# Rotated queries and keys written to DRAM head by head, 32 rows in a transfer

## The chip, the cores and the metric

The kernel runs on one core of a Trainium2 chip. The metric is the device time of one execution in microseconds (us). Three runs of the kernel before gave a median of 3471.29 us (3470.65 to 3471.43).

The core has five engines with instruction queues of their own: PE (TensorE: matmuls and transposes), DVE (VectorE), ACT (ScalarE), POOL (GpSimd) and SP (SyncE). In this kernel every transfer between SBUF and DRAM is issued by SP, in the order of SP's instructions, and moved by the core's 16 DMA engines.

## The reference

A sequence of 2048 tokens with 1024 features goes through two blocks. The first is a gated short convolution and then an attention layer with "stick-breaking" weights. The second is the block that the change touches. Cut to what matters:

```python
h = rms_norm(x, norm_w) * (1 + scale) + shift            # scale, shift, gate from c
u_pool, g_pool, q, k, v, g_attn, qi, ki, wi = split(h @ w_in)
pool_out = pool_mixer(u_pool) * silu(g_pool)
q  = rope(rms_norm(q, q_norm_w))      # 8 heads of 64
k  = rope(rms_norm(k, k_norm_w))      # 2 heads of 64
qi = rope(qi)                         # 8 index heads of 64
ki = rope(ki)                         # 1 index head of 64

def rope(x):                          # rotates the two halves of each head
    x1, x2 = x[..., :32], x[..., 32:]
    return concat([x1 * cos - x2 * sin, x2 * cos + x1 * sin])

def dsa_attention(q, k, v, qi, ki, wi):    # per block of 128 queries
    score = sum_h(relu(qi_h @ ki.T) * wi_h)          # causal
    sel = top_k(score, 256)
    o = softmax(q @ k[sel].T / 8) @ v[sel]

x = x + gate * (concat([pool_out, attn_out]) @ w_out)
```

## The kernel before

The sequence is worked in two halves h of HT = 1024 tokens. Features lie on the 128 partitions, tokens along the row, so a tile of 128 features of one half is 128 rows of 4 KB (512 KB). Matrix products with float32 accuracy take three matmuls per block of weights (`lin`, L112 to L122: high by high, high by low, low by high); a full product of 1024 features and one half is 48 matmuls of 512 columns.

The stages are generators that yield their estimated cost; `merge` (L56) interleaves two of them so that both move in proportion to given totals. A scheduling layer then orders each engine's instructions; the order is fixed when the program is built. The stages by letters:

- `phase_a`, `phase_b`: the convolution block and the projections of the first attention. `phase_c(h)`: stick-breaking attention; it loads queries (`crr<-qst`), keys (`crr<-kst`) and values (`crf<-vst`) through small rings of buffers.
- `phase_d(h)`: output projection of the first block and the norm before the second. `phase_e(h)` (L682): the projections `ki`, `k`, `v`, `qi`, `q`, with rope, written to DRAM for later. `phase_e2`: gates and the pool mixer.
- `f_setup(h)` (L836) loads the second block's keys into SBUF (`keys<-kis`, `keys<-k2s`, `keys<-v2s`), after a small POOL copy (L842). `phase_f`: index scores (L871, L872), top-k search on DVE and ACT, attention (L1147 to L1194); its queries come in as `ffr<-qis` and `ffr<-q2s`. `phase_g`: the last projection.

Around the change, `phase_c(1)` runs merged with `phase_d(0)`, `phase_e(0)`, `phase_e2` of half 0 (L1308, some 1500 to 2100 us into the run), and `phase_d(1)`, `phase_e(1)` run merged with the first part of `phase_f` (L1318, some 2100 to 2500 us).

Rope is in two helpers. `rope_pair` (L646) takes two tiles x and y, the first and second halves of four heads, each 4 heads by 32 rows, and makes four tiles: high and low parts of both results, in the buffers `rb`, `ra`, and twice `xe`. Each of the four goes to DRAM in one transfer of 128 rows (L661). It is called twice per half for `qi` (into `qis`) and twice for `q` (into `q2s`): 32 transfers of 512 KB in all. `rope` (L627) does the same within one tile for `ki` (one head, 32 rows in a transfer of 128 KB, into `kis`) and for `k` (two heads, 64 rows in a transfer of 256 KB, into `k2s`), from the buffers `sw` and `xe`. There are 8 transfers into `k2s` and 8 into `kis`.

Weights of the second half's projections were kept in DRAM by the first half and come back as `fixedr<-kept_w_in`, two transfers of 512 KB for 48 matmuls, into a ring of four buffers (L89), so a load waits until PE has left its buffer.

Completion of SP's transfers is counted in eight semaphores (DMAHW0 to DMAHW7 in the listings below), given out in turn: a transfer that takes a semaphore waits until the transfer that had it before, eight earlier, has landed.

Of the kernel before, what the change touches and what calls it, by code (L numbers as in the profile page):

```python
# [37 lines left out]
def merged(*gens):  # L38

    live = [[0.0, float(total), g] for g, total in gens]  # L40
    while live:
        live.sort(key=lambda e: e[0] / e[1])
        try:
            step = next(live[0][2])
            live[0][0] += step
            yield step
        except StopIteration:
            live.pop(0)


def run(gen):
    for _ in gen:
        pass


def merge(*gens):  # L56
    run(merged(*gens))


def until(gen, stop):  # L60

    while not stop():
        try:
            yield next(gen)
        except StopIteration:
            return


class Build:
# [557 lines left out]
    def rope(self, xe, half, dst):  # L627

        nc = self.nc
        sw = self.t4("sw")[:, :HT]  # L630
        one, two = slice(0, half), slice(half, 2 * half)
        self.dma(sw[one], xe[two])
        self.dma(sw[two], xe[one])
        x, w = xe[: 2 * half], sw[: 2 * half]
        nc.vector.tensor_tensor(x, x, self.cos[: 2 * half], ALU.mult)
        nc.vector.tensor_tensor(w, w, self.sin[: 2 * half], ALU.mult)
        nc.vector.tensor_tensor(x[one], x[one], w[one], ALU.subtract)
        nc.vector.tensor_tensor(x[two], x[two], w[two], ALU.add)
        nc.scalar.activation(w.bitcast(F32R), x, AF.Copy)
        nc.vector.tensor_tensor(x.bitcast(F32R), x, w, ALU.subtract)  # L640
        dst = dst.rearrange("(a t d) s n -> t a d s n", t=2, d=32)
        for t, rows in enumerate((one, two)):
            for i, y in enumerate((w, x)):
                self.dma(dst[t][:, :, i], y[rows])

    def rope_pair(self, x, y, dst):  # L646

        nc = self.nc
        a, b = self.t4("ra")[:, :HT], self.t4("rb")[:, :HT]
        nc.vector.tensor_tensor(a, x, self.cos, ALU.mult)  # L650
        nc.vector.tensor_tensor(b, y, self.sin, ALU.mult)
        nc.vector.tensor_tensor(a, a, b, ALU.subtract)
        nc.scalar.activation(b.bitcast(F32R), a, AF.Copy)
        nc.vector.tensor_tensor(a.bitcast(F32R), a, b, ALU.subtract)
        nc.vector.tensor_tensor(y, y, self.cos, ALU.mult)
        nc.vector.tensor_tensor(x, x, self.sin, ALU.mult)
        nc.vector.tensor_tensor(y, y, x, ALU.add)
        nc.scalar.activation(x.bitcast(F32R), y, AF.Copy)
        nc.vector.tensor_tensor(y.bitcast(F32R), y, x, ALU.subtract)
        for t, i, z in ((0, 0, b), (0, 1, a), (1, 0, x), (1, 1, y)):  # L660
            self.dma(dst[:, t, :, i].rearrange("d a n -> a d n"), z)  # L661

    def head_ms(self, ps, ind, before=None):

# [613 lines left out]
    def build(self):  # L1278
        tc, nc = self.tc, self.nc
        self.scores, self.masks, self.guess, self.r1 = {}, {}, {}, {}  # L1280
        self.kit, self.k2t, self.v2t = {}, {}, {}
        self.exact = False
        self.attended = 0
        self.e1 = self.e2 = False
        self.seen = {}
        pool = tc.tile_pool
        two = lambda a, b: [[i, i + 1] for i in range(a, b, 2)]
        with (
            pool(name="dr", bufs=1, space=DRAM) as self.dr,
            pool(name="cp", bufs=1) as self.cp,  # L1290
            pool(name="sm", bufs=2) as self.sm,
            pool(name="pw", bufs=2) as self.pw,
            pool(name="wk", bufs=1) as self.wk,
            pool(name="xa", bufs=8) as xa,
            pool(name="xb", bufs=8) as xb,
            pool(name="at", bufs=1) as self.at,
            pool(name="xg", bufs=1) as xg,
            pool(name="ps", bufs=1, space=PSUM) as self.ps,
        ):
            self.setup()  # L1300
            self.wide = True
            run(self.phase_a(0, xa, xb))
            merge((self.phase_a(1, xa, xb), 420), (self.adaln(), 9))
            run(self.phase_b(0, xa))
            self.wide = False
            merge((self.phase_b(1, xb), 167), (self.ahead(self.phase_c(0), 2000), 95))
            de = self.chain(self.phase_d(0, xb), lambda: self.phase_e(0), lambda: self.phase_e2([0, 1], self.h2))
            merge((self.ahead(self.phase_c(1), 2000), 260), (de, 300))  # L1308
            self.f_setup(0)
            f = self.phase_f([[b, b + 1] for b in range(0, 16, 2)])  # L1310
            de = self.chain(
                self.phase_d(1, xb),
                lambda: self.phase_e(1),
                lambda: self.f_setup(1) or (),
                lambda: self.phase_e2([2, 3], self.h2),
                lambda: self.done_e2() or (),
            )
            merge((de, 300), (until(f, lambda: self.e2), 230))  # L1318
            g = lambda q: self.chain(
                self.wait(lambda: self.attended >= 4 * q + 4), lambda: self.phase_g(q, xg, self.seen[4 * q + 3])  # L1320
            )
            fill = self.chain(g(0), lambda: g(1), lambda: g(2))
            merge((self.ahead(f, 0), 500), (fill, 400))
            run(self.phase_g(3, xg, self.seen[15]))
            ps = self.bank()
            nc.vector.tensor_tensor(self.dropped, self.dropped, self.due, ALU.not_equal)
            nc.tensor.matmul(ps[0:1, 0:16], self.ones[:, 0:1], self.dropped, start=True, stop=True)
            tot = self.small("tot", 2)[0:1, 0:1]
            nc.vector.tensor_reduce(tot, ps[0:1, 0:16], mybir.AxisListType.X, ALU.add)
            flag = self.small("tot", 2, I32)[0:1, 0:1]  # L1330
            nc.vector.tensor_copy(flag, tot)

            failed = nc.values_load(flag, min_val=0, max_val=P * 16)
            with tc.If(failed > 0):
                self.exact = True
                for h in range(2):
                    self.f_setup(h)
                run(self.phase_f(two(0, 16)))
            with tc.If(failed > 0):
                for q in range(4):  # L1340
                    run(self.phase_g(q, xg))
# [102 lines left out]
```

## Time and profile before

| | |
|---|---|
| Median of the runs | 3471.29 us |
| Profiled execution, its own time | 3474.31 us |
| Span of that execution, first to last instruction | 3472.6 us |
| Granted TensorE clock, mean over the span | 0.962 of full speed |
| Busy: PE, DVE, ACT, POOL | 93%, 65%, 43%, 14% |
| DMA | 438.66 MB, mean 126 GB/s |

A row of the timeline gives the start in us from the span's start, the duration, the engine, the source line, the operation, what it writes and reads (out<-in), and in square brackets how long the engine had been idle before it and what ended that. A row of the waits gives who waited for what: the sum in us, how often, and the longest. A row of the windows gives for one stretch its length, each engine's busy time and number of instructions, the granted TensorE clock, the mean busy share of the 16 DMA engines, and the GB/s that they moved. A "SPq DMA_DIRECT2D" row is the time that SP took to issue transfers, not the time that they took to land.

### The profile page before, as it was taken

Reading aid. Unit: us, or ns where it says so; the run is one execution under the profiler, and the core shown is the slowest. Engines: PE = TensorE matmul, PEld = TensorE weight load, DVE = VectorE, ACT = ScalarE, POOL = GpSimd, SP = SyncE. Lnnn points to the kernel's source line nnn. Section 1 sums busy time; section 2 is a strip of 40 time slices with the busy share of each in tenths; the row PEclk is TensorE's granted clock in tenths of the full one; section 3 lists DMA queues with packets and bytes.
Section 4 is the critical chain, followed back from the end, with each engine's and each line's share of the span. In section 5 each row is a group of like instructions: output and inputs, shape, how many; then the busy total and the mean of one; then the engine's idle time right before and its main releaser. Section 6 shows DMA issues by size and latency. Waiting matters only on the chain. (4 is left out here: it accounts for less than half of the span.)

```text
span 3472.6 us, 49120 instructions
## 1 busy us (share of the span) xinstructions
PE 3222.2 (93%) x17922; PEld 2569.6 (74%) x17922; DVE 2256.2 (65%) x4508; ACT 1482.4 (43%) x2668; POOL 484.3 (14%) x600
## 2 busy tenths in 40 slices
PE   8999999999999999988989998899898898889897
PEld 7888888888787777766767776677676676667675
DVE  5343544553535887788777787897447569888641
ACT  4111421111323444555545555563364365865561
POOL 0000110000100000142021112420200422102002
PEclk9999999999999999989999999899899999989999
DMA  3111442343464545645445444644433542115005
GB/s 108 49 47 52 157 160 83 127 131 107 143 173 140 173 130 153 200 152 139 145 152 178 131 133 137 191 149 145 153 104 107 164 158 95 47 43 174 25 29 174
DMA packets 369231, 438.66 MB, mean 126 GB/s; under 512 B 23504, under 2 KB 269776, under 8 KB 368976
## 3 DMA queue, kind: packets, MB, share of 16 engines
q1 hardware_dynamic: 368976, 435.38, 40.1%
q8 instruction: 145, 2.38, 0.3%
q14 instruction: 110, 0.90, 0.1%
HBM read 308.94 MB, written 124.78 MB: 125 GB/s over the span
## 5 line engine op out<-in xcount | busy, mean ns | idle before, releaser
L119 PE MATMUL lin<-act,fixedr 128*128 128x512 f32 x1488 | 603.6, 406 | 23.5 <-DMA fixedr<-kept_w_in 12.1
L120 PE MATMUL lin<-act,fixedr 128*128 128x512 f32 x1488 | 601.3, 404 | 12.8 <-DVE act L620 10.8
L121 PE MATMUL lin<-act,fixedr 128*128 128x512 f32 x1488 | 598.1, 402 | 0.0
L104 ACT ACTIVATE fixedr<-fixed 128x512 fp32r<-128x512 f32 x295 | 186.9, 634 | 730.0 <-PE lin L120 249.3
L548 DVE TENSOR_TENSOR_SCAN crf<-crf 128x512 f32<-128x512 f32 (+3 forms) x320 | 355.5, 1117 | 64.0 <-ACT crf L545 60.9
L119 PEld LDWEIGHTS lin<-act,fixedr 128*128 128x128 f32 x1488 | 286.8, 193 | 92.2 <-DMA fixedr<-kept_w_in 10.1
L120 PEld LDWEIGHTS lin<-act,fixedr 128*128 128x128 f32 x1488 | 286.0, 192 | 80.5 <-DVE act L620 14.9
L105 DVE TENSOR_TENSOR fixedr<-fixed,fixedr 128x512 fp32r<-128x512 f32 x295 | 204.3, 693 | 204.3 <-ACT fixedr L104 192.7
L121 PEld LDWEIGHTS lin<-act,fixedr 128*128 128x128 f32 x1488 | 285.8, 192 | 63.2
L1149 DVE CUSTOM_DVE_ANT_0 fe<-z,masks 128x512 f32<-128x512 f32 (+3 forms) x320 | 186.8, 606 | 151.7 <-PE z L1148 107.2
L557 ACT COPY crf<-tp 128x512 f32<-128x512 f32 (+3 forms) x320 | 164.5, 532 | 184.0 <-PE tp L555 166.9
L119 PE MATMUL z<-act,fixedr 128*128 128x512 f32 x584 | 231.1, 396 | 10.9 <-ACT fixedr L104 10.9
L538 ACT ACTIVATE crf<-z 128x512 f32<-128x512 f32 (+3 forms) x320 | 174.9, 548 | 136.3 <-PE tp L555 114.4
L121 PE MATMUL z<-act,fixedr 128*128 128x512 f32 x584 | 229.8, 394 | 0.0
L120 PE MATMUL z<-act,fixedr 128*128 128x512 f32 x584 | 229.7, 394 | 0.0
L1172 ACT COPY ff<-tp 128x512 f32<-128x512 f32 (+3 forms) x320 | 160.1, 522 | 156.6 <-PE tp L1170 89.4
L551 POOL TENSOR_TENSOR crf<-crf 128x1 f32<-128x1 f32 x192 | 89.0, 465 | 967.0 <-ACT crf L538 696.7
L881 DVE SCALAR_TENSOR_TENSOR sc<-ff,fixed,sc 128x512 f32<-128x512 f32 (+3 forms) x266 | 176.7, 686 | 59.4 <-ACT ff L874 58.5
L1170 PE MATMUL tp<-fixed,fe 128*128 128x128 f32 x1088 | 185.4, 292 | 30.9 <-ACT fe L1161 21.1
L874 ACT ACTIVATE ff<-z 128x512 f32<-128x512 f32 (+3 forms) x304 | 157.2, 544 | 128.9 <-PE z L872 120.8
L549 DVE TENSOR_TENSOR crf<-crf 128x511 f32<-128x511 f32 (+3 forms) x320 | 200.5, 632 | 11.2 <-DVE crf L548 0.5
L1161 ACT ACTIVATE fe<-fe,fixed 128x128 f32<-128x128 f32 (+15 forms) x128 | 165.7, 1295 | 76.6 <-DVE fixed L1160 75.8
(343 smaller groups left out, 6559.4 us busy)
## 6 DMA issues: line engine op xcount, KB each, us to landing
fixed<-in_w_in_a_dram SPq DMA_DIRECT2D x128, 256.0 KB
fixedr<-kept_w_out SPq DMA_DIRECT2D x64, 512.0 KB
kept_w_in<-fixedr SPq DMA_DIRECT2D x46, 512.0 KB
fixedr<-kept_w_in SPq DMA_DIRECT2D x46, 512.0 KB
crr<-kst SPq DMA_DIRECT2D x80, 256.0 KB
crr<-qst SPq DMA_DIRECT2D x64, 256.0 KB
fixed<-x2d SPq DMA_DIRECT2D x64, 256.0 KB
ffr<-q2s SPq DMA_DIRECT2D x128, 128.0 KB
```

The lines of the kernel that those rows point to most:

```text
L104: nc.scalar.activation(t[:, 0], raw, AF.Copy)
L105: nc.vector.tensor_tensor(t[:, 1], raw, t[:, 0].bitcast(F32), ALU.subtract)
L119: self.nc.tensor.matmul(ps[:, :n], whi[k], a, start=k == 0, stop=False)
L120: self.nc.tensor.matmul(ps[:, :n], whi[k], b, start=False, stop=False)
L121: self.nc.tensor.matmul(ps[:, :n], wlo[k], a, start=False, stop=k == nk - 1)
L538: nc.scalar.activation(s[:, :W], z[:, :W], AF.Sigmoid)
L548: nc.vector.tensor_tensor_scan(er, er, er, left, ALU.mult, ALU.min)
L549: nc.vector.tensor_tensor(s[:, : W - 1], s[:, : W - 1], e[:, 1:W], ALU.mult)
L881: nc.vector.scalar_tensor_tensor(sc[:, c0 : c0 + m], r[:, :m], w, sc[:, c0 : c0 + m], ALU.mult, ALU.add)
L1149: nc.vector.tensor_tensor_reduce(row[:, c0 : c0 + m], z[:, :m], mb[:, c0 : c0 + m], 1.0, NEG, ALU.subtract, ALU.max, mx[:, c : c + 1])
L1161: nc.scalar.activation(row[:, :W], row[:, :W], AF.Exp, bias=nbs, scale=sc, accum_out=den[:, hd : hd + 1])
L1170: nc.tensor.transpose(tp[:, j * P : (j + 1) * P], pe[a][:, k0 : k0 + P], self.ident)
```

## The change

`rope_pair` writes each of its four tiles in four transfers of 32 rows (128 KB), one for each head, instead of one transfer of 128 rows. `rope` does the same: the two heads of `k` go in two transfers of 32 rows instead of one of 64; for `ki`, which has one head, the transfers stay as they were. The places in DRAM and the bytes are the same. SP gets 104 transfers more: 128 for 32 from `rope_pair`, 16 for 8 from `rope`. The total given for `phase_c(1)` in one merge goes from 260 to 250.

```diff
@@ rope
         dst = dst.rearrange("(a t d) s n -> t a d s n", t=2, d=32)
-        for t, rows in enumerate((one, two)):
+        for t in range(2):
             for i, y in enumerate((w, x)):
-                self.dma(dst[t][:, :, i], y[rows])
+                for a in range(half // 32):
+                    r0 = t * half + 32 * a
+                    self.dma(dst[t][a][:, i], y[r0 : r0 + 32])
@@ rope_pair
         for t, i, z in ((0, 0, b), (0, 1, a), (1, 0, x), (1, 1, y)):
-            self.dma(dst[:, t, :, i].rearrange("d a n -> a d n"), z)
+            for hd in range(4):
+                self.dma(dst[:, t, hd, i], z[32 * hd : 32 * hd + 32])
@@ build
-            merge((self.ahead(self.phase_c(1), 2000), 260), (de, 300))
+            merge((self.ahead(self.phase_c(1), 2000), 250), (de, 300))
```

Three places of SP's order show what moves. The sizes at the end of a row's names are the shape that the transfer writes; in brackets is what it waits for. The first place is the first pair of `qi` in half 0. Before:

```order
668 L77 DMA qis_187<-rb 4x32x1024 [waits Activation_49]
669 L77 DMA qis_187<-ra 4x32x1024 [waits DMAHW4_49,DVE_49]
670 L77 DMA qis_187<-xe 4x32x1024 [waits Activation_49]
671 L77 DMA qis_187<-xe 4x32x1024 [waits DMAHW6_49,DVE_49]
672 L77 DMA fixed<-in_w_in_dram 128x4x128 [waits DMAHW7_49,DVE_49]
673 L77 DMA kept_w_in_0_12249<-fixedr 128x1024 [waits DMAHW0_49]
```

With the change, the same place on SP:

```order
676 L77 DMA qis_187<-ra 32x1024 [waits DMAHW3_49,DVE_49]
677 L77 DMA qis_187<-ra 32x1024 [waits DMAHW4_49]
678 L77 DMA qis_187<-ra 32x1024 [waits DMAHW5_49]
679 L77 DMA qis_187<-ra 32x1024 [waits DMAHW6_49]
680 L77 DMA qis_187<-xe 32x1024 [waits DMAHW7_49,Activation_49]
681 L77 DMA qis_187<-xe 32x1024 [waits DMAHW0_49]
682 L77 DMA qis_187<-xe 32x1024 [waits DMAHW1_49]
683 L77 DMA qis_187<-xe 32x1024 [waits DMAHW2_49]
684 L77 DMA qis_187<-xe 32x1024 [waits DMAHW3_49,DVE_49]
```

Each transfer is now four, and each of them takes a semaphore in turn, so the ninth of a pair waits for the first to land; the place in the program is the same.

The second place is the second pair of `qi` in half 0, and the four loads of queries for `phase_c(1)` near it. Before, on SP:

```order
686 L77 DMA qis_187<-ra 4x32x1024 [waits DMAHW5_49,DVE_49]
687 L77 DMA crr<-kst_0_149 64x2x512 [waits DMAHW6_49,PE_49]
688 L77 DMA crr<-kst_0_149 64x2x512 [waits DMAHW7_49]
689 L77 DMA qis_187<-xe 4x32x1024 [waits DMAHW0_49,DVE_49]
690 L77 DMA fixed<-in_w_in_dram 128x4x128 [waits DMAHW1_49,DVE_49]
691 L77 DMA kept_w_in_0_12667<-fixedr 128x1024 [waits DMAHW2_49]
692 L77 DMA crr<-qst_1_158 64x2x512 [waits DMAHW3_49,PE_49]
693 L77 DMA crr<-qst_1_158 64x2x512 [waits DMAHW4_49]
694 L77 DMA crr<-qst_1_158 64x2x512 [waits DMAHW5_49,PE_49]
695 L77 DMA crr<-qst_1_158 64x2x512 [waits DMAHW6_49]
```

With the change, from the first two of the query loads to the last two:

```order
706 L77 DMA crr<-qst_1_158 64x2x512 [waits DMAHW1_49,PE_49]
707 L77 DMA crr<-qst_1_158 64x2x512 [waits DMAHW2_49]
708 L77 DMA qis_187<-ra 32x1024 [waits DMAHW3_49,DVE_49]
...
719 L77 DMA qis_187<-xe 32x1024 [waits DMAHW6_49]
720 L77 DMA fixed<-in_w_in_dram 128x4x128 [waits DMAHW7_49,DVE_49]
721 L77 DMA kept_w_in_0_12635<-fixedr 128x1024 [waits DMAHW0_49]
722 L77 DMA crr<-qst_1_158 64x2x512 [waits DMAHW1_49,PE_49]
723 L77 DMA crr<-qst_1_158 64x2x512 [waits DMAHW2_49]
```

Two of the query loads now stand ahead of 12 of the writes (rows 708 to 719), the other two behind all 16 of the pair.

The third place is the end of `phase_e(1)`, where `f_setup(1)` loads the keys. Before, on SP:

```order
1027 L77 DMA q2s_186<-xe 4x32x1024 [waits DMAHW3_49,Activation_49]
1028 L77 DMA sg_198<-fixed 128x512 [waits DMAHW4_49,DVE_49]
1029 L77 DMA fixedr<-kept_w_in_4_13506 128x1024 [waits DMAHW5_49,PE_49]
1030 L77 DMA q2s_186<-xe 4x32x1024 [waits DMAHW6_49,DVE_49]
1031 L77 DMA keys<-kis_204 64x1024 [waits DMAHW7_49,DMAHW1_49,Pool_49]
1032 L77 DMA keys<-kis_204 64x1024 [waits DMAHW0_49]
```

With the change:

```order
1128 L77 DMA q2s_186<-xe 32x1024 [waits DMAHW7_49]
1129 L77 DMA fixedr<-kept_w_in_4_13486 128x1024 [waits DMAHW0_49,PE_49]
1130 L77 DMA keys<-kis_204 64x1024 [waits DMAHW2_49,DMAHW1_49,Pool_49]
1131 L77 DMA keys<-kis_204 64x1024
1132 L77 DMA q2s_186<-xe 32x1024 [waits DMAHW3_49,DVE_49]
1133 L77 DMA q2s_186<-xe 32x1024 [waits DMAHW4_49]
```

The loads of `kis` now stand ahead of the last four writes of the last pair. Elsewhere in the stretch of the two merges, matmuls of the two stages change places by a few to a few dozen rows on PE, and DVE's rows likewise; both stages start and end at the same rows as before to within a few tens.

## Rows read from the trace of the kernel before

**Rows 1.** The page, busy time of each engine over the whole span

```profile
PE 3222.2 (93%) x17922; PEld 2569.6 (74%) x17922; DVE 2256.2 (65%) x4508; ACT 1482.4 (43%) x2668; POOL 484.3 (14%) x600
```

**Rows 2.** Waits of PE from 1600 to 2520 us, those that a transfer ended

```profile
PE z L535 <- DMA crr<-qst: 15.5, 3, 13.9
PE lin L119 <- DMA fixedr<-kept_w_in: 12.1, 3, 5.8
PE z L871 <- DMA keys<-kis: 11.4, 1, 11.4
PE z L871 <- DMA ffr<-qis: 9.1, 4, 3.4
...
PE o L563 <- DMA crf<-vst: 4.7, 2, 2.7
```

**Rows 3.** Timeline of PE around the longest of these waits

```profile
1770.80 0.40 PE L120 MATMUL lin<-act,fixedr 128*128 128x512 f32 x1
1771.04 0.39 PE L121 MATMUL lin<-act,fixedr 128*128 128x512 f32 x1
1785.30 0.45 PE L535 MATMUL z<-crr 128*128 128x128 f32 x1 [13.87 <-DMA crr<-qst]
...
1786.29 0.63 PE L120 MATMUL lin<-act,fixedr 128*128 128x512 f32 x1
1786.72 0.63 PE L121 MATMUL lin<-act,fixedr 128*128 128x512 f32 x1
```

**Rows 4.** Windows: engines, granted clock, DMA share and GB/s of short stretches

```profile
1774.00:1784.00 10.00, 0.00 (x0) 0.00 (x0) 0.00 (x0) 0.00 (x0) 0.00 (x0) 0.56 0.78 232
1786.00:1789.00 3.00, 3.00 (x9) 2.32 (x9) 0.00 (x0) 0.00 (x0) 0.00 (x0) 0.52 0.20 75
...
2440.00:2444.00 4.00, 3.65 (x9) 2.88 (x10) 0.41 (x2) 1.06 (x1) 0.00 (x0) 0.50 0.25 103
2494.00:2502.00 8.00, 0.00 (x0) 0.00 (x0) 0.00 (x0) 0.00 (x0) 0.00 (x0) 0.59 0.53 185
2503.00:2509.00 6.00, 5.89 (x16) 4.76 (x17) 1.39 (x3) 1.74 (x4) 2.17 (x2) 0.50 0.90 261
...
1613.00:1614.00 1.00, 1.00 (x11) 0.64 (x13) 1.00 (x4) 1.00 (x3) 0.00 (x0) 1.00 0.26 61
1614.00:1615.00 1.00, 1.00 (x17) 0.83 (x14) 1.00 (x5) 0.41 (x1) 0.35 (x1) 1.00 0.89 201
1726.00:1728.00 2.00, 2.00 (x10) 1.63 (x9) 1.90 (x3) 1.11 (x2) 0.00 (x0) 1.00 0.26 104
1692.00:1693.00 1.00, 1.00 (x6) 0.81 (x5) 0.96 (x2) 1.00 (x3) 0.38 (x1) 1.00 0.13 53
```

**Rows 5.** Timeline of SP: the issue of transfers ahead of that wait

```profile
1753.59 0.55 SPq L77 DMA_DIRECT2D qis<-rb  x1
...
1759.14 3.10 SPq L77 DMA_DIRECT2D crr<-kst  x2
1762.34 1.14 SPq L77 DMA_DIRECT2D qis<-xe  x1
1765.37 3.23 SPq L77 DMA_DIRECT2D fixed<-in_w_in_dram  x1
1768.65 3.36 SPq L77 DMA_DIRECT2D kept_w_in<-fixedr  x1
1772.10 5.47 SPq L77 DMA_DIRECT2D crr<-qst  x4
```

**Rows 6.** Timeline of SP: two of the transfers of 32 rows

```profile
1612.99 0.80 SPq L77 DMA_DIRECT2D kis<-sw  x2
```

**Rows 7.** Waits of SP, 1778 to 1783 us and 2392 to 2408 us

```profile
SPq L77 <- DMA qis<-xe: 2.4, 1, 2.4
...
SPq L77 <- DMA qis<-xe: 14.4, 2, 7.5
```

**Rows 8.** Timeline of POOL: the copy that stands before the loads of the keys

```profile
2488.72 0.55 POOL L842 CAST keys<-fixed 128x1 fp32r<-128x1 f32 x4 [9.39 <-DMA q2s<-ra]
```

## The prediction

> **What bounds the kernel now.** I read the busy times first: PE is busy 93% of the span, DVE 65%, ACT 43% [rows 1]. So time goes up or down with PE's idle time and PE's clock. Next I read what PE waits for, only in the stretch where rotated tiles are written, 1600 to 2520 us. The largest causes are not DVE or ACT but transfers [rows 2]: query loads of `phase_c` 15.5 us, returning weights 12.1 us, the loads of the keys 11.4 us, index queries 9.1 us, values of `phase_c` 4.7 us.
>
> Then I asked what these transfers stood behind. While the tiles of a `qi` pair drain, the 16 DMA engines are on average 0.26 busy and move 104 GB/s; while `k` drains, 0.13 and 53 GB/s; while `ki`, whose transfers have 32 rows, drains, 0.89 and 201 GB/s [rows 4]. 0.26 is 4 of 16 engines and 0.13 is 2 of 16. That matches the shapes in the SP order: 4x32x1024 for a pair, 2x32x1024 for `k`, 32x1024 for `ki`. So a pair's four tiles, 2.10 MB, take 2.10 MB / 104 GB/s = about 20 us on a quarter of the engines, and `k`'s four transfers (1.05 MB at 53 GB/s) also 20 us on two engines. Everything issued meanwhile needs all 16 engines and must get past those few.
>
> The longest wait shows the chain. SP issues the pair's writes from 1753.59 us; from 1759 us each further issue takes 1 to 3.4 us, and the query loads go out at 1772.10 us [rows 5]. PE, whose last matmul before started at 1771.04 us, stands until 1785.30 us [rows 3]. From 1774 to 1784 us no engine does anything, with the DMA engines 0.78 busy [rows 4]. A write issued at 1762.34 us had not landed at 1778 us, since SP then waited 2.4 us more for it [rows 5, 7]. The second pattern is SP standing still: 14.4 us in two waits for `qis<-xe` to land, just ahead of loads of weights [rows 7]. The third is the keys: POOL's small copy waits 9.39 us for `q2s<-ra` [rows 8], SP loads the keys only then, behind the rest of the backlog, and all engines are idle from 2494 to 2502 us [rows 4].
>
> **The change, part by part.**
>
> *The idle time of PE that goes.* I count the four causes that stand behind such writes: 15.5 + 12.1 + 11.4 + 4.7 = 43.7 us [rows 2]. I don't count the 9.1 us for `ffr<-qis`: those four waits lie where no rotated tile is being written.
>
> *The clock that comes back.* After a long idle time PE runs at the lower of its levels, 1.2 instead of 2.4 GHz: matmuls start 0.43 us apart (1786.29 to 1786.72) instead of 0.24 [rows 3]. Three stretches of work after these waits show a granted clock of 0.52 for 3 us, 0.50 for 4 us and 0.50 for 6 us [rows 4]; at full clock they would be shorter by 1.4 + 2.0 + 3.0 = 6.4 us. Together 50.1 us is the most that the writes cost now.
>
> *What stays.* Two transfers of 32 rows (262 KB) moved in two windows, 61 + 201 GB/s over 1 us each, while the engines were busy for 0.26 + 0.89 = 1.15 us [rows 4]: 228 GB/s. So a pair's 16 transfers would need 2.10 / 0.228 = 9.2 us of all engines instead of 20 us of four. At the longest wait, 22 issues lie between the first write and the last two query loads in the new order. A 32-row transfer takes 0.40 us to issue (two in 0.80 [rows 6]), the others are taken at the 0.55 us of the first write [rows 5]: 16 x 0.40 + 6 x 0.55 = 10 us, so the loads go out near 1764 us instead of 1772 us and land well before 1771 us. I leave 1 us there. For the returning weights I leave 2 us, for the values and the short query waits 2 us. The keys keep the most: POOL's copy still waits for writes of the last pair to land, and the loads follow it; I leave 4 us, and 1 us of clock. Left over: 10 us. The bounds are 0 (all goes) and, if only the places where every engine is idle come back, 50.1 - 22 = 28 us (below).
>
> *What is added.* SP issues 104 transfers more: 144 x 0.40 = 58 us against 40 x 0.55 = 22 us [rows 5, 6], so 36 us over some 900 us. This lies beside SP's waits; it costs nothing as long as what queues behind a group of writes (weights, queries, keys) is not needed at once. If that cover is gone it is the slower rival below. The engine time per tile goes up too: 4 engines for 5 us is 20 engine-us; 4 x 0.575 x 16 is 37. Over the 32 tiles that is 17 x 32 / 16 = 34 us of all engines, beside a DMA load that leaves more than half of the time free on average. I cost both at nothing; their ends are 0 and the rival's price.
>
> *What is moved.* The total of 250 instead of 260 and the longer list of transfers shift rows of PE and DVE against each other. No row of before prices that. The nearest is the 9.1 us of waits for `ffr<-qis` [rows 2], a wait of the kind that order alone makes; I take 0 and keep 9 us to both sides.
>
> *The sum.* 3474.3 us of the profiled execution (span 3472.6 and 1.7 around it) - 50.1 + 10 + 0 = 3434.2 us. The median of the runs lies 3.0 us below the profiled execution, so 3431 us.
>
> **A rule that speaks against it.** In the rows the small transfers are not ruled by a fixed cost: two of 128 KB kept the engines 0.89 busy [rows 4]. The Trainium skill, "DMA: Bandwidth & Descriptors", section "Rules for kernel authors", says the opposite of this change: many small transfers should be coalesced into one large one. Its section on the anatomy of one DMA puts the fixed part, mostly completion, at about 2.0 us for the GpSimd path. By that page 104 more transfers are an estimated 208 us if nothing overlaps, and 26 us if eight are always in flight. The trace agrees that a write takes long to be reported, but here it is the backlog of four engines that made it 16 us. The rule's mechanism in this kernel is the slower rival.
>
> **The rivals.**
>
> *Half comes back.* With the transfers quick, another engine limits the stage. Certain to come back are only the stretches where all engines were idle: 10 us and 8 us [rows 4], and the clock after them, 1.4 + 3.0: about 22 us. That gives 3449 us. For it: DVE is at 65% overall and each stage hands work back and forth. Against it: in 2440 to 2444 us DVE was busy 0.41 of 4 us [rows 4], so there too DVE had room.
>
> *The eight semaphores hold SP (slower).* Sixteen writes share eight semaphores, so if a 128 KB write takes L to be reported, a pair holds SP for 16 L / 8 = 2 L. The weights on hand feed PE for 48 matmuls of 0.24 us [rows 3], 11 us. With L = 10 us SP is held 20 us, PE starves 9 us, eight pairs cost 72 us against the 50 gained: 3471 + 22 = 3493 us. It decides from 2 L = 11 + 50/8, L = 8.7 us on. For it: `qis<-xe` took over 16 us [rows 5, 7]. Against it: that was the four-engine backlog, and `ki`'s transfers were through the engines within 2 us of their first issue [rows 4, 6].
>
> *No change.* The moved rows open a wait as large as what is gained, or the 32-row transfers also run on few engines. The second is as good as excluded by 0.89 [rows 4]; the first would need five times the 9.1 us. 3471 us.
>
> **How the numbers follow.** Forecast 0.66 (own range 3412 to 3445 us: 50.1 + 9 gained and 26 gained), half 0.17, no change 0.07, slower 0.10. What this measurement can tell from no change is about 0.2%, 7 us. The half case lies wholly on the faster side, so faster 0.83, same 0.07, slower 0.10. The range goes from 3410 us (all of 50.1, 9 for the order, and 2 for rounding) up to 3460 us (the half case with 9 us against it); the last two cases are left out, and little else.
>
> **What would show it.** Right: DMA share well above 0.26 while `qis` and `q2s` are written, no window with all engines idle near the second `qi` pair, waits of PE for `crr<-qst`, `fixedr<-kept_w_in` and `keys<-kis` together below 12 us, issues behind the writes back to 0.3 to 0.6 us each, SP's waits for `qis` gone. Wrong on the sum: those waits gone but DVE or ACT named in their place (half). Wrong altogether: SP waiting for `qis` or `q2s` in many short waits with PE waiting for weights behind them (slower), or a DMA share still near 0.26.

## The result, and the profile after

The changed kernel takes 3412.4 us (median of four runs; 3404.53 to 3413.05), the kernel before 3470.97 us beside it: a ratio of 0.9827, 95% interval [0.981, 0.9844], 58.6 us less. The forecast was 40 us less, 3431 us; the measured time lies inside the range of 3410 to 3460 us, near its lower end. The profiled execution of the changed kernel took 3404.53 us, 8 us below its median, so a sum over its trace comes out that much too large; where it matters, a second trace stands beside it.

Busy times of the engines, which answer to [rows 1]:

```profile
PE 3193.5 (94%) x17922; PEld 2544.7 (75%) x17922; DVE 2254.1 (66%) x4508; ACT 1482.5 (44%) x2666; POOL 488.1 (14%) x600
```

PE issued the same 17922 matmuls and was busy for 28.7 us less: a matmul took less time on average. The rest of the difference of the spans (3472.6 - 3402.8 = 69.8 us), 41.1 us, is idle time.

PE's waits for transfers, 1600 to 2520 us, as in [rows 2]:

```profile
PE z L874 <- DMA ffr<-qis: 9.3, 6, 3.6
...
PE z L535 <- DMA crr<-qst: 0.8, 1, 0.8
```

These two are all. Returning weights, keys and values are gone from the list, and of 43.7 us in the four causes 0.8 us is left. The wait that the forecast left out, for `ffr<-qis`, is as it was.

DMA share and GB/s while the first `qi` pair of half 0 is written (windows, columns as in [rows 4]):

```profile
1707.00:1709.00 2.00, 2.00 (x10) 1.60 (x9) 2.00 (x3) 2.00 (x6) 0.26 (x1) 1.00 0.58 131
1709.00:1711.00 2.00, 2.00 (x10) 1.62 (x9) 2.00 (x4) 1.83 (x3) 0.00 (x0) 1.00 0.93 266
1711.00:1713.00 2.00, 2.00 (x13) 1.65 (x12) 2.00 (x4) 0.64 (x3) 0.00 (x0) 1.00 0.93 273
1713.00:1715.00 2.00, 2.00 (x23) 1.48 (x22) 1.97 (x3) 1.45 (x4) 0.49 (x1) 1.00 0.93 264
```

The engines are 0.93 busy instead of 0.26 and move 264 to 273 GB/s instead of 104. SP's issues around the second pair, the place of [rows 3, 5] (timeline of SP):

```profile
1745.65 1.72 SPq L77 DMA_DIRECT2D qis<-rb  x4
1747.72 1.28 SPq L77 DMA_DIRECT2D crr<-qst  x2
1749.48 1.72 SPq L77 DMA_DIRECT2D qis<-ra  x4
1751.29 4.14 SPq L77 DMA_DIRECT2D qis<-xe  x8
1755.53 1.38 SPq L77 DMA_DIRECT2D fixed<-in_w_in_dram  x1
1756.95 0.51 SPq L77 DMA_DIRECT2D kept_w_in<-fixedr  x1
1757.56 1.43 SPq L77 DMA_DIRECT2D crr<-qst  x2
```

The last two query loads go out at 1757.56 us, 12 us after the first write; before it was 1772.10 us, 18.5 us after. Writes cost 0.43 to 0.52 us each to issue, and an issue behind them takes 0.5 to 1.4 us, not 3.4. From 1770 to 1840 us PE is busy without a gap at a granted clock of 1.00, the stretch that held the 13.87 us wait. SP no longer waits for any `qis` or `q2s` write to land, and POOL's copy before the keys [rows 8] does not wait:

```profile
2429.64 0.55 POOL L845 CAST keys<-fixed 128x1 fp32r<-128x1 f32 x4
```

The groups of DMA issues give the median from issue to landing (last column, us), the L of the slower rival:

```profile
qis<-xe SPq DMA_DIRECT2D x32, 128.0 KB, 2.7
q2s<-xe SPq DMA_DIRECT2D x32, 128.0 KB, 3.4
qis<-rb SPq DMA_DIRECT2D x16, 128.0 KB, 2.2
```

It is 2.2 to 3.4 us, far below the 8.7 us from which that rival would have decided.

To see where the time came from, I cut both spans at three places: at 1500 us (the one cut by time; the kernels are nine matmuls apart there), at the first index score (`z<-keys,ffr`), and at the first matmul after PE's long wait for `pp`, which both kernels have (27.54 and 27.05 us). Windows of before:

```profile
1500.00:2147.30 647.30, 595.09 (x3860) 469.15 (x3858) 517.86 (x718) 346.43 (x674) 131.57 (x208) 0.96 0.46 142
2147.30:2704.03 556.73, 473.89 (x2395) 378.98 (x2395) 401.48 (x1128) 267.01 (x504) 103.94 (x106) 0.91 0.43 140
2704.03:3472.60 768.57, 679.54 (x4516) 527.96 (x4516) 509.24 (x1416) 412.27 (x684) 155.36 (x147) 0.95 0.32 102
```

Windows of the changed kernel:

```profile
1500.00:2115.80 615.80, 586.09 (x3869) 461.71 (x3868) 516.14 (x720) 349.94 (x677) 137.45 (x207) 0.98 0.49 148
2115.80:2638.42 522.62, 465.40 (x2395) 371.33 (x2396) 403.03 (x1128) 265.12 (x502) 103.69 (x106) 0.93 0.48 149
2638.42:3402.80 764.38, 672.31 (x4516) 521.35 (x4516) 509.16 (x1416) 412.21 (x684) 153.92 (x147) 0.95 0.32 103
```

The first stretch holds half 0's writes and loses 31.5 us, the second half 1's and loses 34.1 us; 4.2 us come from the end. In the two stretches PE's idle time falls by 48.1 us (22.5 + 25.6) and its busy time, for the same work to within nine matmuls, by 17.5 us (9.0 + 8.5).

### The profile page after: what moved, and what is told of

Its sections match the earlier page's. It is cut to its first block, busy times and chain, and to the rows that moved or that the text cites. A ratio compares the mean times of both kernels' runs of the same rounds, so it can differ in the third digit from the quotient of the medians.

```text
span 3402.8 us, 49280 instructions
## 1 busy us (share of the span) xinstructions
PE 3193.5 (94%) x17922; PEld 2544.7 (75%) x17922; DVE 2254.1 (66%) x4508; ACT 1482.5 (44%) x2666; POOL 488.1 (14%) x600
## 5 line engine op out<-in xcount | busy, mean ns | idle before, releaser
L119 PEld LDWEIGHTS lin<-act,fixedr 128*128 128x128 f32 x1488 | 283.2, 190 | 78.5 <-DVE x1r L599 8.4
L120 PEld LDWEIGHTS lin<-act,fixedr 128*128 128x128 f32 x1488 | 282.4, 190 | 72.1 <-DVE act L620 8.9
L121 PEld LDWEIGHTS lin<-act,fixedr 128*128 128x128 f32 x1488 | 282.3, 190 | 62.1 <-issue 0.2
L551 POOL TENSOR_TENSOR crf<-crf 128x1 f32<-128x1 f32 x192 | 96.4, 504 | 931.9 <-ACT crf L538 672.6
```

The source lines that it names most:

```text
L119: self.nc.tensor.matmul(ps[:, :n], whi[k], a, start=k == 0, stop=False)
L120: self.nc.tensor.matmul(ps[:, :n], whi[k], b, start=False, stop=False)
L121: self.nc.tensor.matmul(ps[:, :n], wlo[k], a, start=False, stop=k == nk - 1)
```

## Experiments

Theory A: the outermost size of the shape that a transfer writes sets how many of the 16 DMA engines work on it, and what PE pays is the backlog on those few. B: the order made by the total does it. C: many small pieces help as such. D, E, F stand in the expectations. Seven of the eleven kernels have the total 245, so that only the transfers (and the order that follows from them) differ between them; 240, 255 and 270, with 260 (before) and 250 (the change), are the order's own series, and one kernel changes half 0 alone at 260.

**The change and the order apart.** The whole change with 245, and the transfers of before with 245:

```diff
-            merge((self.ahead(self.phase_c(1), 2000), 260), (de, 300))
+            merge((self.ahead(self.phase_c(1), 2000), 245), (de, 300))
```

> The change, with the total of phase_c(1) at 245 instead of 250: the same transfers, another order. Theory A (the gain is the drain of rotated tiles moving from 4 or 2 DMA engines to all 16, worth about 50 us, and the order only adds some 9 us either way): 3412 us +- 10, PE's waits for crr<-qst, kept_w_in and keys<-kis together below 5 us. Theory B (a good part of the 59 us, some 25 us, is the particular order that 250 gave): this order would lose it, 3430 to 3440 us.

> The transfers of the kernel before, with the total of phase_c(1) at 245 instead of 260: order alone. Theory A: 3471 us +- 10, and PE still waits 40 us or so for crr<-qst, kept_w_in, keys<-kis and crf<-vst. Theory B: 25 us faster than before, about 3446 us.

Measured: 3408.68 us, ratio 0.9822 [0.9805, 0.9838], and with the transfers of before 3454.82 us, 0.9956 [0.9941, 0.9971]. So at one total the transfers are worth 46 us, and the order of 245 takes 17 us off the kernel before. The first hits A (3412 us +- 10). The second misses both: A expected 3471 us +- 10 and some 40 us of waits for queries, weights, keys and values, B 3446 us. Order is worth more than the 9 us that A gave it. PE's waits in the kernel with old transfers and 245, 1600 to 2620 us:

```profile
PE z L871 <- DMA keys<-kis: 10.5, 1, 10.5
PE lin L119 <- DMA fixedr<-kept_w_in: 9.5, 4, 3.5
PE z L871 <- DMA ffr<-qis: 5.9, 3, 3.4
PE z L535 <- DMA crr<-qst: 1.0, 1, 1.0
```

The four causes come to 21 us instead of 43.7. The new order alone removed the 13.9 us wait for queries, by moving those loads: they now go out between 1755.84 and 1764.22 us, among the writes of the pair that start at 1754.37 us. It left the keys and the weights. Its windows (old transfers, 245):

```profile
1500.00:2131.30 631.30, 591.05 (x3864) 464.05 (x3862) 515.45 (x718) 350.01 (x677) 133.21 (x207) 0.97 0.47 144
2131.30:2687.65 556.35, 477.19 (x2395) 378.91 (x2396) 403.36 (x1128) 265.66 (x502) 104.62 (x106) 0.91 0.44 140
```

and those of the whole change at 245:

```profile
1500.00:2124.20 624.20, 588.11 (x3872) 462.97 (x3871) 516.54 (x721) 349.91 (x677) 129.01 (x207) 0.98 0.50 147
2124.20:2649.18 524.98, 465.55 (x2395) 373.49 (x2395) 400.98 (x1128) 265.47 (x502) 104.90 (x106) 0.93 0.48 148
```

Order has already taken 16 us from the first stretch, so the transfers add 7 us there and 31 us in the second. Of these 38 us, 24 us are idle time of PE and 14.6 us its busy time.

**Number of engines against number of pieces.** First, two heads in a transfer (2x32x1024): more transfers than before, on fewer engines.

```diff
-            self.dma(dst[:, t, :, i].rearrange("d a n -> a d n"), z)
+            for hd in range(0, 4, 2):
+                self.dma(dst[:, t, hd : hd + 2, i].rearrange("d a n -> a d n"), z[32 * hd : 32 * hd + 64])
```

> rope_pair writes two heads in a transfer (2x32x1024, 256 KB), so 64 transfers instead of 32 or 128; k as in the change; total 245. Theory A (the outermost size of the shape sets the number of DMA engines): 2 engines, DMA share near 0.13 and 53 GB/s while a pair drains, 40 us per pair instead of 20, so slower than the kernel before: 3490 to 3600 us. Rival C (smaller pieces help by themselves, because loads get between them): between the change and before, 3430 to 3450 us.

Measured: 3568.55 us, 1.0284 [1.0266, 1.0301]. DMA share and GB/s while such a pair drains:

```profile
1718.00:1724.00 6.00, 6.00 (x42) 4.77 (x41) 4.35 (x5) 3.02 (x7) 0.52 (x2) 1.00 0.13 53
1724.00:1730.00 6.00, 6.00 (x31) 4.55 (x31) 4.04 (x5) 2.77 (x6) 0.93 (x2) 1.00 0.13 53
```

The share is 2 of 16, and PE waits for weights and keys:

```profile
PE lin L119 <- DMA fixedr<-kept_w_in: 51.9, 7, 13.1
PE z L874 <- DMA keys<-kis: 22.8, 1, 22.8
```

Twice the pieces on half the engines make the kernel 97 us slower than the kernel before, and 114 us slower than its transfers at the same total. Second, `qis` laid out in DRAM so that the first and second halves of a head alternate row by row: the 128 rows of a tile are then evenly spaced and go in one transfer whose outermost size is 128; `k` likewise in one of 64, `q` head by head.

```diff
-        self.qis = [dr.tile([64, 8, 2, HT], F32R, name=f"qis{h}") for h in range(2)]
+        self.qis = [dr.tile([512, 2, HT], F32R, name=f"qis{h}") for h in range(2)]
...
-            self.dma(dst[:, t, :, i].rearrange("d a n -> a d n"), z)
+            if len(dst.shape) == 4:
+                self.dma(dst[t][:, i], z)
+            else:
+                for hd in range(4):
+                    self.dma(dst[t][:, hd, i], z[32 * hd : 32 * hd + 32])
...
-        return t[:, 4 * g : 4 * g + 4].rearrange("(t d) a s n -> d t a s n", t=2)
+        if len(t.shape) == 3:
+            return t[256 * g : 256 * g + 256].rearrange("(r t) s n -> t r s n", t=2)
+        return t[:, 4 * g : 4 * g + 4].rearrange("(r t) a s n -> t r a s n", t=2)
```

> The two halves of a head are interleaved row by row in DRAM, so that one transfer of 128 evenly spaced rows (128x1024, 512 KB) holds four heads of qi, and one of 64 rows both heads of k; q head by head, 32 rows, as in the change; total 245. 56 transfers fewer than in the change. Theory A: all 16 engines also for these, same time as the change with 245, within 10 us, SP with less to issue; DMA share near 1 while qi drains. Rival C (pieces of 32 rows are what helps): the waits near the qi pairs come back, 13.9 us and 3 to 4 us of the returning weights, so about 20 us slower than the change with 245.

Measured: 3412.93 us, 0.9834 [0.9817, 0.985], not distinguishable from the change at 245, with 56 transfers fewer. The first `qi` tile, 512 KB in one transfer, and the half microsecond after it:

```profile
1712.00:1712.50 0.50, 0.50 (x4) 0.41 (x3) 0.50 (x1) 0.00 (x0) 0.00 (x0) 1.00 0.93 385
1712.50:1713.00 0.50, 0.50 (x5) 0.41 (x4) 0.50 (x2) 0.00 (x0) 0.00 (x0) 1.00 0.98 410
1713.00:1713.50 0.50, 0.50 (x9) 0.33 (x9) 0.50 (x1) 0.29 (x1) 0.00 (x0) 1.00 0.62 254
1713.50:1714.00 0.50, 0.50 (x14) 0.50 (x12) 0.50 (x2) 0.20 (x1) 0.00 (x0) 1.00 0.05 16
```

In these 2 us 0.53 MB are moved, which is the one tile; while it is moved the engines are 0.93 to 0.98 busy at 385 to 410 GB/s, and then they stand idle. So one transfer of 128 rows fills all the engines, as A said. PE has no wait for `crr<-qst`, weights or keys from 1600 to 2720 us, so the waits that C expected near the `qi` pairs are not there. Shares of 2, 4 and 16 engines thus go with 3569, 3455 and 3409 us at one total, and on 16 engines 56 pieces fewer give the same time to within 4 us (3413 us). A holds, C falls.

**Pairs alone.** `rope_pair` as in the change, `k` on two engines as before.

```diff
-            self.dma(dst[:, t, :, i].rearrange("d a n -> a d n"), z)
+            for hd in range(4):
+                self.dma(dst[:, t, hd, i], z[32 * hd : 32 * hd + 32])
```

> rope_pair alone is changed (its tiles head by head); k stays in transfers of 2x32x1024 on two engines; total of phase_c(1) 245. Theory A (what counts is how long few engines have a backlog, wherever it is): k's four writes are 20 us of backlog per half beside four times 20 us for qi and q, a fifth of it, so a fifth of the 46 us stays: 3418 us (3412 to 3425). Theory D (a backlog costs only where loads that PE needs soon stand behind it; near k there are none): 3409 us, within 3 us of the whole change at 245, and no PE wait for a transfer over 3 us near the k writes.

Measured: 3421.46 us, 0.9849 [0.9829, 0.9869]: 13 us over the whole change at 245. The intervals of the two ratios just overlap; the runs themselves do not (3415 to 3424 us against 3408 to 3411 us). SP's timeline shows the price of `k` in half 1,

```profile
2333.75 9.10 SPq L77 DMA_DIRECT2D k2s<-xe  x2
2342.95 2.04 SPq L77 DMA_DIRECT2D fixedr<-kept_w_in  x2
```

and PE's timeline who pays it:

```profile
2357.99 0.77 PE L119 MATMUL lin<-act,fixedr 128*128 128x512 f32 x1 [3.27 <-DMA fixedr<-kept_w_in]
```

Two issues took 9.10 us behind the backlog, and the weights behind them came 3.27 us late. In half 0 the price comes by way of another engine. A weight load issued behind `k`'s writes takes 6.08 us to issue, ACT waits 8.19 us for that load, and PE waits 4.96 us for ACT (rows of SP, ACT and PE):

```profile
1669.31 6.08 SPq L77 DMA_DIRECT2D fixed<-in_w_in_dram  x1
1689.72 0.63 ACT L104 ACTIVATE fixedr<-fixed 128x512 fp32r<-128x512 f32 x1 [8.19 <-DMA fixed<-in_w_in_dram]
1691.17 0.80 PE L535 MATMUL z<-crr 128*128 128x512 f32 x1 [4.96 <-ACT crf L538]
```

A wait of PE for ACT can thus be a late transfer too. From 1690 to 1695 us PE then has a granted clock of 0.50. That is A, not D, though D's bounds (3409 us within 3 us, no wait over 3 us) are passed by little in the row of half 1. By the two stretches cut as above, 10 us of the 13 lie in the second (534.9 us against 525.0) and 3 us in the first (627.1 against 624.2); what makes up the 10 us beyond the 3.27 us wait is not shown.

**How much the order decides.** Old transfers with 255 and 270, the change with 240.

> Transfers as before, only the total of phase_c(1) 255 instead of 260 (245 gave 3455 us, 260 gives 3471 us). Theory A with order as chance (which loads stand behind a backlog decides what it costs): a time anywhere from 3445 to 3480 us, with the difference from before found in PE's waits for crr<-qst, kept_w_in and keys<-kis. Theory B (the smaller total is in itself the better mix of the two stages): between the two, 3460 to 3468 us, with those waits as before.

> Transfers as before, total of phase_c(1) 270. Theory A with order as chance: 3445 to 3490 us, the sum of PE's waits for crr<-qst, kept_w_in, keys<-kis and crf<-vst following the time. Theory B (smaller total is better): above 3475 us, with those waits as before.

> The whole change with a total of 240 instead of 250 (3412 us) or 245 (3409 us). Theory A with order as chance: with no backlog left the order costs little, 3404 to 3417 us, and PE's waits for crr<-qst, kept_w_in, keys<-kis together below 3 us. Theory B (smaller total is better, 16.7 us from 260 to 245): 3400 to 3405 us.

Measured: 3480.42 us, 1.0019 [1.0009, 1.0029]; 3444.51 us, 0.992 [0.9903, 0.9936]; and 3402.56 us, 0.9803 [0.9782, 0.9824], the fastest of all kernels here. With the old transfers the totals 245, 255, 260, 270 give 3455, 3480, 3471, 3445 us, without a direction; B falls as a rule on the total. With the new ones 240, 245, 250 give 3403, 3409, 3412 us: 10 us of swing instead of 36, over a smaller range of totals. These three do rise with the total, and 240 lies in B's range and 1 us below A's (3404 to 3417 us), so among the new transfers B's direction is not excluded. The old ones at 255 and 270 lie within half a microsecond of the ends of A's wide ranges, 255 just above its own and 270 just below. PE's waits for queries, weights, keys and values go along only roughly: with 255

```profile
PE z L871 <- DMA keys<-kis: 11.5, 1, 11.5
PE lin L119 <- DMA fixedr<-kept_w_in: 10.5, 3, 4.0
PE z L535 <- DMA crr<-qst: 10.1, 2, 6.6
PE z L871 <- DMA ffr<-qis: 9.1, 3, 3.8
PE o L563 <- DMA crf<-vst: 7.6, 1, 7.6
```

they sum to 39.7 us, 4 us less than before [rows 2], at a time 9 us longer; with 270 to 29.6 us. With 240 and the new transfers PE has none of these waits.

**The two halves apart.** A flag picks the form by half, here for half 0 alone:

```diff
+            if not split:
+                self.dma(dst[:, t, :, i].rearrange("d a n -> a d n"), z)
+                continue
+            for hd in range(4):
+                self.dma(dst[:, t, hd, i], z[32 * hd : 32 * hd + 32])
...
+            self.rope_pair(*pair, self.heads(self.qis[h], g), h == 0)
```

> Head by head only in phase_e(1), the second half of the sequence; in phase_e(0) the transfers are as before; total of phase_c(1) 245. Old transfers at 245 took 3455 us, the whole change at 245 3409 us. Theory A, place by place: between these two the stretch from 1500 us to the first index score (z<-keys,ffr) differs by 7 us (631 and 624 us) and the stretch from there to the long wait of PE for pp by 31 us (556 and 525 us). So with the second half alone the first stretch stays near 631 us, the second falls to 525 us, and the time is 3417 us (3411 to 3424). Theory E (what comes back is PE's clock and idle time everywhere alike, half from each half of the sequence): 3432 us, with the second stretch near 540 us.

> Head by head only in phase_e(0), the first half; total of phase_c(1) 245. Theory A, place by place: the first stretch falls to 624 us, the second stays near 556 us, PE's waits for kept_w_in and keys<-kis after 2150 us stay (near 15 us together): 3447 us (3440 to 3454). Theory E: 3432 us.

> Head by head only in phase_e(0), with the total of phase_c(1) at 260 as in the kernel before. Theory A: the transfers alone, without a new total, take away the 13.9 us wait for crr<-qst, so the first stretch falls from 647 us to near 625 us and the time to 3450 us (3443 to 3458). Theory F (the first stretch was helped by the total of 245 or 250, the transfers there only went along): the first stretch stays above 640 us and the time above 3463 us.

Measured: half 1 alone 3422.01 us, 0.9857 [0.984, 0.9873]; half 0 alone 3431.86 us, 0.9892 [0.9876, 0.9909]; half 0 alone with 260 3453.18 us, 0.9956 [0.9939, 0.9972]. The second stretch in these three, in this order:

```profile
2138.90:2665.03 526.13, 467.33 (x2395) 372.57 (x2396) 402.61 (x1128) 265.15 (x502) 107.31 (x106) 0.93 0.48 148
```

```profile
2118.80:2672.49 553.69, 475.73 (x2395) 379.21 (x2395) 399.87 (x1128) 265.90 (x502) 102.22 (x106) 0.90 0.45 141
```

```profile
2127.50:2681.02 553.52, 471.64 (x2395) 376.10 (x2395) 402.11 (x1128) 267.62 (x504) 103.24 (x106) 0.92 0.44 141
```

It is 526 us with half 1 changed and 554 us without, as A said (525 and 556), not 540 for both (E). Half 0's place is the first stretch: 638.9, 618.8 and 627.5 us. At 260, with nothing else changed, it falls from 647.3 to 627.5 us and the time by 17 us (F falls). Half 1 alone came within A's range, though its first stretch is 8 us longer than the 631 us of the same transfers at 245. Half 0 alone at 245 was 15 us faster than A's 3447 us and took just the time that E named, 3432 us. Of these 15 us, 5 lie in the first stretch (618.8 us, not 624), 2 in the second, and 7 behind it (757.6 us against 764.5), where nothing is changed. So E is refuted by the second stretch, not by the time. The place of each gain is shown; the sizes don't add up to better than about 10 us.

## Why the prediction was right, and where its sizes were off

**The mechanism was right.** The signs named beforehand are there: 0.93 instead of 0.26, no gap near the second pair, three causes together 0.8 us where below 12 was named, no SP wait for `qis`. The issues behind the writes came down too, but to 0.5 to 1.4 us, not to the 0.3 to 0.6 us named. A page of the Trainium skill states the first step of the mechanism, the number of engines: "DMA: Bandwidth & Descriptors", in "Why a DMA increments its semaphore by 16 and not by 1", says that the number of engines is the largest up to 16 that divides the slowest dimension (not of size 1) on both sides. The trace agrees with shares of 0.13 for 2 and 0.26 for 4 [rows 4], and 0.93 for 32.

**"The idle time of PE that goes", 43.7 us: right**, 42.9 us of it went (0.8 left). All of PE's idle time in the two stretches fell by 48.1 us, in the change at 245 by 39.5 us (first stretch 52.2 to 36.1, second 82.8 to 59.4), so other waits neither ate it nor added much to it.

**"What stays", 10 us: too much.** Of its 9 us of idle time 0.8 us stayed. The largest piece, 4 us for the keys, failed because POOL's copy did not have to wait any more for `q2s<-ra` (issued at 2425.25 us, 4.4 us before the copy), and the loads of `kis` went out at 2430.22 us ahead of the last four writes.

**"The clock that comes back", 6.4 us: too little.** It counted three stretches after waits [rows 4]. PE's busy time in the two stretches fell by 17.5 us, in the change at 245 by 15.3 us, and by 14.6 us between old and new transfers at one total (591.05 + 477.19 against 588.11 + 465.55). Windows of before where the count had nothing, or less:

```profile
1620.00:1640.00 20.00, 18.54 (x108) 14.55 (x108) 14.15 (x21) 9.62 (x20) 6.59 (x14) 0.83 0.13 41
1780.00:1800.00 20.00, 14.70 (x90) 12.00 (x91) 6.58 (x10) 6.06 (x13) 0.68 (x3) 0.78 0.33 96
1880.00:1900.00 20.00, 18.05 (x107) 14.46 (x105) 12.49 (x20) 7.68 (x16) 0.60 (x3) 0.91 0.60 198
```

In the changed kernel the granted clock is 1.00 in all three stretches of time (other work may stand there), and from 2300 to 2600 us it is 1.00 with PE busy 300.00 of 300 us. That the account closes can be worked out: busy time times granted clock, summed over windows of 4 us, is 3136 us before, 3138 us after, and 3135 to 3142 us in the eleven experiments. The work is fixed; the time is that plus idle time plus what the clock takes. What made the clock fall at each of these places is not shown: the 3.0 us idle time before 1620.77 us was ended by POOL, not by a transfer.

**"What is added", 0: right.** 56 transfers fewer gained nothing, and writes land 2.2 to 3.4 us after their issue.

**"What is moved", 0 within 9 us: the bounds were too narrow, and the value stays open.** Orders of the old transfers lie from 28 us faster to 8 us slower than the kernel before beside them. What 250 did by itself can't be told: neither the whole change at 260 nor the old transfers at 250 was run. The change at three totals gives 3403 to 3412 us, so its own order is not a lucky one; but 260 is a slow order for the old transfers. Against their fastest order here (270, 3445 us) the changed kernel is 32 us faster, not 58.6, so a part of the 58.6 us may be the leaving of a slow order, which the forecast put at nothing.

Together: about 9 us less stays and 9 to 11 us more clock comes back than forecast, which is the size of the 18.6 us between 40 and 58.6. Both misses go the same way, so the forecast did not come into its range by errors that cancel. The account is good to some 10 us: the last stretch, where these helpers write nothing, took 757.6 to 768.6 us in the single traces of the thirteen kernels (768.6 before, 764.4 with the change, 760.1 with the change at 245), and why is open. PE's busy time for the same 4516 matmuls there is 679.5 us before, 682.0 us with old transfers at 245, and 672.3 and 671.5 us in the change at 250 and 245.

**The rivals.** Half comes back (3449 us): false, PE ran without a gap where the waits had been. Eight semaphores: false, since the median from issue to landing is 2.2 to 3.4 us and SP has no wait for a `qis` or `q2s` write (its bound of 8.7 us is 8.6 by the figures given, which changes nothing). No change: false.

## What to carry to other kernels

Read the DMA share while one kind of transfer drains: a share near 2/16 or 4/16 names a shape whose outermost size is 2 or 4, and the cost stands not at that transfer but at the loads that SP issues behind it. Put a large size outermost, by splitting or by the layout in DRAM (32 and 128 rows filled the engines here); more pieces on fewer engines made it worse. Compare the change with more than one order of the old kernel, since one order can be a slow one. Price a wait that goes with the slow clock too: compare PE's busy time for the same number of matmuls, not only the few rows after the wait.

## What was not expected of the hardware

The 32-row transfers keep the engines 0.93 busy at 264 to 273 GB/s, one 128-row transfer 0.93 to 0.98 busy at 385 to 410 GB/s; by these rates I estimate 1.3 us for a tile instead of 2. Whether the engines or SP set the slower pace is not shown: SP issued the 16 writes of that pair from 1707.09 to 1714.57 us, and 2.10 MB in these 7.5 us is 280 GB/s. The faster tile gained no time here. A 128-row transfer whose rows are evenly spaced was issued in 0.32 us (0.32 to 0.54 us for the single ones near it), against 0.55 us for 4x32x1024 [rows 5]:

```profile
1711.21 0.32 SPq L77 DMA_DIRECT2D qis<-rb  x1
```

Behind a backlog on two engines, four issues took 21 us (two heads in a transfer):

```profile
1712.55 21.20 SPq L77 DMA_DIRECT2D qis<-xe  x4
```

The spread of the runs does not follow the backlog. The old transfers took 3447 to 3472 us over 10 runs at 245, but 3440 to 3445 us over 4 at 270; the new ones 3408 to 3411 us at 245 and 3401 to 3411 us at 240, over 4 each.
